# Two-layer hybrid encoder: layer 1's probabilities times values as plain fp32 products instead of three split products

## The chip, the cores and the metric

The kernel runs on one core of one Trainium2 chip. The metric is the device time of one execution in microseconds (us). A core has several engines with instruction queues of their own: TensorE (PE in the profile, its weight loads PEld), VectorE (DVE), ScalarE (ACT), GpSimd (POOL), and SyncE (SP), whose queue here issues the DMAs. Each queue is worked off in the order that was fixed when the kernel was built; an instruction that has to wait holds up what stands behind it on the same engine.

## The reference

The input x is 2048 x 1024, float32. Layer 0 is an attention layer of two mixers (a sliding window and a chunked attention with a position bias) with an input and an output projection; the change does not touch it. Layer 1 is differential attention with 8 heads, each with two queries and keys of 64 numbers and one value of 128:

```python
q1, q2, k1, k2 = ...            # projected, RMS-normed, rotated
s1, s2 = (q1 @ k1.T) / 8, (q2 @ k2.T) / 8     # chunk-causal mask: key chunk <= query chunk
a = softmax(s1) - lam * softmax(s2)
o = a @ v                        # per head: 2048 x 2048 times 2048 x 128
o = rms_norm(o, subln_g) * (1 - lambda_init)
y = (o * silu(gate)) @ w_out     # and x + y
```

The change is about `o = a @ v` and about how v is kept between the projection and that product.

## The kernel before

The work of layer 1 has two stages. The first (`_project`, lines 224 to 488) norms x, splits x and the weights into a high and a low part, and projects. The second (`_mix1`, lines 845 to 1187) does the attention, the gate projection and the output projection, woven into one another.

**Split products.** A float32 number is kept as two tiles of type fp32r: H, the rounded copy, and L, the difference to the original. A product of two such numbers is three fp32r products, HH + HL + LH, which add up in the same PSUM bank (`mm3`, lines 211 to 216, and lines 954 to 956 by hand). H is made by an ACT copy, L by a subtraction on DVE or POOL.

**Values in the projection.** The columns of v are the two groups of kind "cv" (line 291), each of 512 columns. For each of 16 blocks of 128 rows, ACT copies the PSUM bank into vH (line 483), DVE subtracts to vL (line 484), and two DMAs on SP's queue store both to HBM (lines 485 and 486): 32 of each in all. After the projection, `load_v` (lines 1026 to 1035) fetches for a head and a block of 512 keys one tile of vH and one of vL, with a DMA each, from a pool of four places for each.

**Scores.** `scores` (line 880) takes a head h and a block b of 512 queries. For each of the 4 rows of 128 queries and both softmaxes, and each chunk of up to 512 keys, PE makes a score bank with two products (lines 901 and 902; there are 4 score banks), DVE takes the row maximum (line 905), ACT the exponential into an SBUF tile (line 908). The tiles are named P0 (19 places, pool `pp`) and P1 (6 places). POOL scales both by their softmax sums and adds them (lines 924, 933, 934; every fifth time DVE does the last step, line 931). The result stays in the P0 tile and is the 128 x 512 piece of `a`; the P1 tile comes free.

**Values in the attention.** `values` (line 937) takes, for each of the (b + 1) * 4 tiles of 128 keys, the pieces of `a` of the 4 query rows, transposes them on PE (line 947) into a PSUM bank (2 banks, tag "tr"), lets ACT copy the bank to ptH (line 950) and DVE subtract to ptL (line 951), each with 3 places, and adds three products to the one output bank O (lines 954 to 956). In the block on the diagonal the later key tiles meet fewer queries, so the width falls from 512 to 384, 256 and 128. Over 8 heads and 4 blocks there are 320 key tiles, 224 of them 512 wide and 32 of each smaller width. `gate` (line 965) takes the finished bank: a copy, the norm with a sum over partitions by a plain fp32 product of the squares with a matrix of ones (line 981), and the gate.

**The order.** `pace` (line 48) runs the scores of one (head, block) ahead of the values of an earlier one by `LAG1` units (30 to 36), and lets the side work follow by a table (`STAGES1`): 256 steps of the gate projection (line 1059), then the output projection (line 1082). The order of (head, block) is: all heads with blocks 0 and 1, then all heads with block 2, then all with block 3. The last part of the output projection follows when the last head is done.

Of the kernel before, what the change touches and what calls it, by code (L numbers as in the profile page):

```python
# [10 lines left out]
F32 = mybir.dt.float32  # L11
F32R = mybir.dt.float32r
AF = mybir.ActivationFunctionType
ALU = mybir.AluOpType
# [4 lines left out]
P = 128  # L19
# [12 lines left out]
def f32(ap):  # L32
    return ap.bitcast(F32)
# [52 lines left out]
class Trunk:  # L86
# [16 lines left out]
    def scratch(self):  # L103
        dram = self.ctx.enter_context(self.tc.tile_pool(name="scr", bufs=1, space=DRAM))

        def d(name, shape):
            return dram.tile(shape, F32, tag=name, name=name)

        self.s0 = {
            "aqH": d("aqH", [4, P, S]), "aqL": d("aqL", [4, P, S]),  # L110
            "akH": d("akH", [1, P, S]), "akL": d("akL", [1, P, S]),
            "av": d("av", [S, 2 * 192]),
            "bqH": d("bqH", [4, P, S]), "bqL": d("bqL", [4, P, S]),
            "bkH": d("bkH", [4, P, S]), "bkL": d("bkL", [4, P, S]),
            "bv": d("bv", [S, 8 * 128]),
            "g": d("g0", [D, S]),
            "woH": d("wo0H", [KT, P, D]), "woL": d("wo0L", [KT, P, D]),
        }
        self.s1 = {
            "qH": d("qH", [8, P, S]), "qL": d("qL", [8, P, S]),  # L120
            "kH": d("kH", [8, P, S]), "kL": d("kL", [8, P, S]),
            "vH": d("vH", [S, D]), "vL": d("vL", [S, D]),
            "g": d("g1", [D, S]), "o": d("o1", [D, S]),
            "hH": d("hH", [KT, P, S]), "hL": d("hL", [KT, P, S]),
            "woH": d("wo1H", [KT, P, D]), "woL": d("wo1L", [KT, P, D]),
            "wgH": d("wgH", [8, P, KT, P]), "wgL": d("wgL", [8, P, KT, P]),
        }
        self.x1 = d("x1", [S, D])
# [95 lines left out]
    def _project(self, es, layer):  # L224
# [194 lines left out]
        for half in range(2):  # L419
# [13 lines left out]
            for gi, (kind, c0, width, o) in enumerate(groups):  # L433
                w = ready or weights(c0, width)
                ready = None
                if gi >= self.AHEAD:
                    next(ahead, None)
                for bi, b in enumerate(blocks):
                    if kind == "gate":
                        for c in range(4):  # L440
                            if half == 1 and gi == len(groups) - 1 and bi * 4 + c >= 8 - self.LATE:
                                self.late.append((b, c, w, h[bi], o["r0"]))
                                continue
                            ps = pmm.tile([P, 512], F32, tag="mm", name=n + "mg")
                            for k in range(KT):
                                self.mm3(
                                    ps, w[0][k][:, c * P:(c + 1) * P], w[1][k][:, c * P:(c + 1) * P],
                                    h[bi][0][:, k, :], h[bi][1][:, k, :], k == 0, k == KT - 1,
                                )
                            gt = self.yp.tile([P, 512], F32, tag="xr", name=n + "gt", bufs=2)  # L450
                            nc.scalar.activation(gt, ps, AF.Exp, scale=-1.0)
                            nc.scalar.activation(gt, gt, AF.Ln, bias=self.one)
                            nc.scalar.activation(gt, gt, AF.Exp, scale=-1.0)
                            nc.vector.tensor_tensor(gt, ps, gt, ALU.mult)
                            nc.sync.dma_start(
                                s["g"][o["r0"] + c * P:o["r0"] + (c + 1) * P, b * BLK:(b + 1) * BLK], gt
                            )
                        continue
                    xs = []
                    for j in range(NTB):  # L460
                        t = b * NTB + j
                        tok = slice(t * P, (t + 1) * P)
                        ps = project_tile(h[bi], j, w, width)
                        if kind == "qk":
                            xs.append(normed(ps, 8, o["tab"], t))
                        elif kind == "akv":
                            xs.append(normed(ps, 2, o["tab"], t))
                            vt = sb.tile([P, 2, 192], F32R, tag="sq", name=n + "vt")
                            pv = ps[:, 128:256].rearrange("p (h d) -> p h d", d=HD)
                            nc.scalar.activation(vt[:, :, 0:64], pv, AF.Copy)  # L470
                            nc.vector.tensor_tensor(vt[:, :, 64:128], pv, f32(vt[:, :, 0:64]), ALU.subtract)
                            nc.scalar.activation(vt[:, :, 128:192], pv, AF.Copy)  # L472
                            nc.sync.dma_start(s["av"][tok, :].rearrange("p (h c) -> p h c", h=2), f32(vt))
                        elif kind == "bv":
                            vt = xp.tile([P, 4, 4, HD], F32R, tag="vb", name=n + "vb", bufs=2 - layer)
                            pv = ps.rearrange("p (h e d) -> p h e d", h=4, e=2)
                            nc.scalar.activation(vt[:, :, 0::3, :], pv, AF.Copy)
                            nc.vector.tensor_tensor(vt[:, :, 1:3, :], pv, f32(vt[:, :, 0::3, :]), ALU.subtract)
                            nc.sync.dma_start(s["bv"][tok, :], f32(vt).rearrange("p a e d -> p (a e d)"))
                        else:  # L480
                            vH = gp.tile([P, 512], F32R, tag="vH", name=n + "vH")
                            vL = gp.tile([P, 512], F32R, tag="vL", name=n + "vL")
                            nc.scalar.activation(vH, ps, AF.Copy)
                            nc.vector.tensor_tensor(vL, ps, f32(vH), ALU.subtract)
                            nc.sync.dma_start(s["vH"][tok, o["c0"]:o["c0"] + 512], f32(vH))
                            nc.sync.dma_start(s["vL"][tok, o["c0"]:o["c0"] + 512], f32(vL))
                    if xs:
                        pairs_out(xs, 4 if kind == "qk" else 1, b, o)

# [355 lines left out]
    def _mix1(self, es):  # L845
# [5 lines left out]
        ld = pool("ld", 2)  # L851
        yp = pool("y", 2 * KT)
        vp = pool("v", 4)
        pp = pool("pp", 19)
        kp = pool("kp", 4)
        sb = pool("sb", 2)
        NS, NTR, NO, NM = self.BANKS1
# [22 lines left out]
        def scores(h, b, q, K, res, then):  # L880
# [4 lines left out]
            for j in range(NTB):  # L885
# [9 lines left out]
                for m in range(2):  # L895
                    chunks = []
                    for z, (c, ce) in enumerate(cuts):
# [5 lines left out]
                        if ce == nk:  # L903
                            nc.vector.memset(ps[0:HD, wd - 64:], NEG)
                        nc.vector.tensor_reduce(nm[:, m, z:z + 1], ps, AX.X, ALU.max, negate=True)  # L905
                        chunks.append((sb if m else pp).tile([P, 512], F32, tag=f"P{m}", name=n + f"P{m}", bufs=6 if m else None))
                        acc = la[:, m, z:z + 1] if nb > 1 else l[:, m:m + 1]
                        nc.scalar.activation(chunks[z][:, :wd], ps, AF.Exp, bias=nm[:, m, z:z + 1], accum_out=acc)  # L908
                        then(j, m, z)
# [27 lines left out]
        def values(h, b, res):  # L937
# [3 lines left out]
            for kt in range(nkt):  # L941
# [3 lines left out]
                kk = (kt % 4) * P  # L945
                for j in range(j0, NTB):
                    nc.tensor.transpose(tp[:, (j - j0) * P:(j - j0 + 1) * P], us[j][kt // 4][:, kk:kk + P], self.ident)  # L947
                H = sb.tile([P, 512], F32R, tag="ptH", name=n + "ptH", bufs=3)
                L = sb.tile([P, 512], F32R, tag="ptL", name=n + "ptL", bufs=3)
                nc.scalar.activation(H[:, :wd], tp[:, :wd], AF.Copy)  # L950
                nc.vector.tensor_tensor(L[:, :wd], tp[:, :wd], f32(H[:, :wd]), ALU.subtract)  # L951
                o = O[:, j0 * P:]
                vH, vL = (v[:, kk:kk + P] for v in res["v"][kt // 4])
                mm(o, vH, H[:, :wd], start=(kt == 0), stop=False, skip_group_check=True)  # L954
                mm(o, vL, H[:, :wd], start=False, stop=False, skip_group_check=True)  # L955
                mm(o, vH, L[:, :wd], start=False, stop=(kt == nkt - 1), skip_group_check=True)  # L956
                if kt == 2:
                    while normal:
                        normal.pop(0)()
# [65 lines left out]

        def load_v(h, i):
            tok = slice(i * BLK, (i + 1) * BLK)
            vs = []
            for part in ("vH", "vL"):
                v = vp.tile([P, BLK], F32R, tag=part, name=n + part)  # L1030
                nc.sync.dma_start(
                    f32(v).rearrange("p (t c) -> p t c", t=NTB), s[part][tok, h * P:(h + 1) * P].rearrange("(t p) c -> p t c", p=P)
                )
                vs.append(v)
            return vs

        room = self.last_hidden
        ended = set()
# [64 lines left out]
        def projected_last():  # L1103
# [7 lines left out]
                pairs.append((t[:, 0, :], t[:, 1, :]))  # L1111
            for i in range(4):
                pairs.append([
                    pl.tile([P, BLK], F32R, tag=tag, name=n + "w" + tag, bufs=6 if tag == "P1" else None)
                    for pl, tag in tags[1][2 * i:2 * i + 2]
                ])
            for k in range(KT):
# [110 lines left out]
```

## Time and profile before

| | before |
|---|---|
| median of 3 runs | 2894.28 us (2891.87 to 2897.59) |
| the profiled execution | 2896.36 us |
| its span, first to last instruction | 2894.3 us |
| mean granted TensorE clock over the span | 0.974 |
| PE busy in the span | 2709.4 us |
| DMA, whole kernel | 549.01 MB |
| projection of layer 1, about | 1195 to 1782 us of the span |
| attention of layer 1 with gate and output projection, about | 1782 to 2894 us |

How to read the profile: a group's line gives the source line, the engine, the operation, the tiles (output<-inputs, with a letter ahead for the stage: p1 is the projection of layer 1, c its attention), the shape and the number of instructions, then busy time and mean duration of one, then the idle time of the engine just before them and what ended most of it. So `cptL<-ctr,cptH` is line 951. A matrix product lasts longer in the record than the distance to the next one, because its way through the array overlaps with that of the next; the cost of one in a dense run is the distance between starts. A plain fp32 product is recorded as two MATMULs. In a table of windows the columns are busy time and count of each engine, the granted TensorE clock, the share of DMA time and GB/s.

### The profile page before, as it was taken

The numbers are of one execution on the slowest core, as the hardware profiler recorded it, in microseconds if no ns is written. First come the engines' busy times: TensorE is split into PE (matmuls) and PEld (weight loads), VectorE is DVE, ScalarE is ACT, GpSimd is POOL, SyncE is SP. The second block draws the span as 40 slices with busy tenths as digits, with TensorE's granted clock in tenths as the row PEclk, the third lists the DMA queues.
The fourth block names the chain that finished last, engine by engine and source line by source line (L and its number), as shares of the span: only waits on it lengthen the run. The fifth ranks groups of instructions, "written<-read, shape, count | busy, mean of one in ns | idle before, by whom it ended". The sixth has DMA issues, their size and how long they took to land. (4 is left out here: it accounts for less than half of the span.)

```text
span 2894.3 us, 45144 instructions
## 1 busy us (share of the span) xinstructions
PE 2709.4 (94%) x13704; PEld 2239.5 (77%) x13704; DVE 1970.7 (68%) x4875; ACT 1593.4 (55%) x4135; POOL 1588.1 (55%) x1740
## 2 busy tenths in 40 slices
PE   7999999999899998999999998998999999898999
PEld 5888888887788887777788887776777777676777
DVE  7752385257788875598638842578888888676772
ACT  4443543367766664343343322577776767666762
POOL 3541251334535353367645741567787878877872
PEclk9999999999999999999999999999999999899999
DMA  5673343738976765557884455978778777465553
GB/s 161 221 240 138 117 136 127 222 112 227 235 185 185 189 182 151 207 198 248 268 294 148 126 180 155 283 227 230 206 205 234 190 219 223 138 181 165 154 166 114
DMA packets 398722, 549.01 MB, mean 190 GB/s; under 512 B 46480, under 2 KB 178320, under 8 KB 398480
## 3 DMA queue, kind: packets, MB, share of 16 engines
q1 hardware_dynamic: 398480, 546.14, 63.3%
q8 instruction: 109, 1.79, 0.3%
q14 instruction: 133, 1.09, 0.1%
HBM read 380.58 MB, written 165.41 MB: 189 GB/s over the span
## 5 line engine op out<-in xcount | busy, mean ns | idle before, releaser
L908 ACT ACTIVATE cP<-cS,cnm 128x512 f32<-128x512 f32 (+3 forms) x640 | 399.3, 631 | 152.1 <-DVE cnm L905 109.0
L905 DVE TENSOR_REDUCE cnm<-cS 128x1 f32<-128x512 f32 (+3 forms) x640 | 373.8, 600 | 59.6 <-PE cS L902 54.5
L924 POOL TENSOR_SCALAR cP<-cP,crl,ce 128x512 f32<-128x512 f32 (+3 forms) x288 | 213.8, 755 | 207.3 <-DVE crl L919 73.4
L214 PE MATMUL p1mm<-p1wH,p1hH 128*128 128x512 f32 x768 | 302.8, 396 | 0.7 <-ACT p1wH L308 0.7
L215 PE MATMUL p1mm<-p1wL,p1hH 128*128 128x512 f32 x768 | 302.9, 395 | 0.4 <-POOL p1wL L310 0.4
L216 PE MATMUL p1mm<-p1wH,p1hL 128*128 128x512 f32 x768 | 303.1, 395 | 0.0
L901 PE MATMUL cS<-ck,cqd 128*128 128x512 f32 (+3 forms) x640 | 264.4, 416 | 40.2 <-ACT cP L908 28.1
L310 POOL TENSOR_TENSOR p0wL<-p0ws,p0wH 128x512 fp32r<-128x512 f32 (+1 forms) x124 | 148.7, 1229 | 269.0 <-ACT p0wH L308 266.7
L934 POOL TENSOR_TENSOR cP<-cP,cP 128x512 f32<-128x512 f32 (+3 forms) x256 | 286.6, 1141 | 1.2
L214 PE MATMUL p0mm<-p0wH,p0hH 128*128 128x512 f32 (+1 forms) x640 | 239.6, 376 | 4.7 <-ACT p0vt L472 4.0
L310 POOL TENSOR_TENSOR p1wL<-p1ws,p1wH 128x512 fp32r<-128x512 f32 x128 | 167.5, 1328 | 138.6 <-ACT p1wH L308 97.6
L902 PE MATMUL cS<-ck,cql 128*128 128x512 f32 (+3 forms) x640 | 236.3, 373 | 5.3 <-DMA cql<-qL 5.3
L216 PE MATMUL p0mm<-p0wH,p0hL 128*128 128x512 f32 (+1 forms) x640 | 239.2, 374 | 1.9 <-DVE p0hL L336 1.9
L215 PE MATMUL p0mm<-p0wL,p0hH 128*128 128x512 f32 (+1 forms) x640 | 239.8, 375 | 0.0
L951 DVE TENSOR_TENSOR cptL<-ctr,cptH 128x512 fp32r<-128x512 f32 (+1 forms) x320 | 190.8, 599 | 53.4 <-ACT cptH L950 52.7
L950 ACT ACTIVATE cptH<-ctr 128x512 fp32r<-128x512 f32 (+1 forms) x320 | 170.3, 538 | 80.2 <-PE ctr L947 78.9
L901 PEld LDWEIGHTS cS<-ck,cqd 128*128 128x128 f32 x640 | 123.1, 193 | 79.0 <-ACT cP L908 53.6
L947 PE MATMUL ctr<-ident,cP 128*128 128x128 f32 x1088 | 177.9, 278 | 6.4 <-POOL cP L934 3.9
L933 POOL TENSOR_SCALAR cP<-cP,crl,ce 128x512 f32<-128x512 f32 (+3 forms) x230 | 177.4, 781 | 5.1 <-DVE crl L920 5.1
L215 PEld LDWEIGHTS p1mm<-p1wL,p1hH 128*128 128x128 f32 x768 | 145.3, 189 | 29.8 <-POOL p1wL L310 0.8
L214 PEld LDWEIGHTS p1mm<-p1wH,p1hH 128*128 128x128 f32 x768 | 145.4, 189 | 29.6 <-ACT p1wH L308 1.0
L216 PEld LDWEIGHTS p1mm<-p1wH,p1hL 128*128 128x128 f32 x768 | 145.3, 189 | 29.2 <-issue 0.2
(311 smaller groups left out, 7744.7 us busy)
## 6 DMA issues: line engine op xcount, KB each, us to landing
p1ws<-in_od_w_in_dram SPq DMA_DIRECT2D x56, 512.0 KB, 4.9
p0ws<-in_ev_w_in_dram SPq DMA_DIRECT2D x48, 512.0 KB, 4.5
ck<-kH SPq DMA_DIRECT2D x144, 128.0 KB, 4.1
ck<-kL SPq DMA_DIRECT2D x144, 128.0 KB, 4.2
cvH<-vH SPq DMA_DIRECT2D x72, 256.0 KB, 4.6
cvL<-vL SPq DMA_DIRECT2D x72, 256.0 KB, 4.4
cqd<-qH SPq DMA_DIRECT2D x128, 128.0 KB, 4.6
cql<-qL SPq DMA_DIRECT2D x128, 128.0 KB, 4.7
```

The source lines that it names most:

```text
L214: mm(ps, aH, bH, start=first, stop=False)
L215: mm(ps, aH, bL, start=False, stop=False)
L216: mm(ps, aL, bH, start=False, stop=last)
L310: low.tensor_tensor(l[:, :width], ws[:, k, :width], f32(h[:, :width]), ALU.subtract)
L901: mm(ps, qd[:, m, js], kt[:, :wd], start=True, stop=False)
L902: self.anchor = mm(ps, ql[:, m, js], kt[:, :wd], start=False, stop=True).ins
L905: nc.vector.tensor_reduce(nm[:, m, z:z + 1], ps, AX.X, ALU.max, negate=True)
L908: nc.scalar.activation(chunks[z][:, :wd], ps, AF.Exp, bias=nm[:, m, z:z + 1], accum_out=acc)
L924: nc.gpsimd.tensor_scalar(p1, p1, rl[:, 0:1], e1, ALU.mult, ALU.mult)
L934: nc.gpsimd.tensor_tensor(p1, p1, p2, ALU.add)
L947: nc.tensor.transpose(tp[:, (j - j0) * P:(j - j0 + 1) * P], us[j][kt // 4][:, kk:kk + P], self.ident)
L951: nc.vector.tensor_tensor(L[:, :wd], tp[:, :wd], f32(H[:, :wd]), ALU.subtract)
```

## The change

Values are stored and loaded once, as float32. The transposed probabilities are copied once, as float32, and not split: for two of three key tiles by ACT and for every third by DVE. One plain fp32 product takes the place of the three fp32r products. The copy has 6 places where ptH and ptL had 3 each. The P0 tiles get 20 places instead of 19, the P1 tiles 8 instead of 6; the value tiles have 4 places where vH and vL had 4 each.

```diff
-            "vH": d("vH", [S, D]), "vL": d("vL", [S, D]),
+            "v": d("v", [S, D]),
...
-                            vH = gp.tile([P, 512], F32R, tag="vH", name=n + "vH")
-                            vL = gp.tile([P, 512], F32R, tag="vL", name=n + "vL")
-                            nc.scalar.activation(vH, ps, AF.Copy)
-                            nc.vector.tensor_tensor(vL, ps, f32(vH), ALU.subtract)
-                            nc.sync.dma_start(s["vH"][tok, o["c0"]:o["c0"] + 512], f32(vH))
-                            nc.sync.dma_start(s["vL"][tok, o["c0"]:o["c0"] + 512], f32(vL))
+                            vt = gp.tile([P, 512], F32, tag="v", name=n + "v", bufs=3)
+                            nc.scalar.activation(vt, ps, AF.Copy)
+                            nc.sync.dma_start(s["v"][tok, o["c0"]:o["c0"] + 512], vt)
...
-        pp = pool("pp", 19)
+        pp = pool("pp", 20)
...
-                        chunks.append((sb if m else pp).tile([P, 512], F32, tag=f"P{m}", name=n + f"P{m}", bufs=6 if m else None))
+                        chunks.append((sb if m else pp).tile([P, 512], F32, tag=f"P{m}", name=n + f"P{m}", bufs=8 if m else None))
...
-                H = sb.tile([P, 512], F32R, tag="ptH", name=n + "ptH", bufs=3)
-                L = sb.tile([P, 512], F32R, tag="ptL", name=n + "ptL", bufs=3)
-                nc.scalar.activation(H[:, :wd], tp[:, :wd], AF.Copy)
-                nc.vector.tensor_tensor(L[:, :wd], tp[:, :wd], f32(H[:, :wd]), ALU.subtract)
-                o = O[:, j0 * P:]
-                vH, vL = (v[:, kk:kk + P] for v in res["v"][kt // 4])
-                mm(o, vH, H[:, :wd], start=(kt == 0), stop=False, skip_group_check=True)
-                mm(o, vL, H[:, :wd], start=False, stop=False, skip_group_check=True)
-                mm(o, vH, L[:, :wd], start=False, stop=(kt == nkt - 1), skip_group_check=True)
+                T = sb.tile([P, 512], F32, tag="pt", name=n + "pt", bufs=6)
+                if kt % 3:
+                    nc.scalar.activation(T[:, :wd], tp[:, :wd], AF.Copy)
+                else:
+                    nc.vector.tensor_copy(T[:, :wd], tp[:, :wd])
+                v = res["v"][kt // 4][:, kk:kk + P]
+                mm(O[:, j0 * P:], v, T[:, :wd], start=(kt == 0), stop=(kt == nkt - 1), skip_group_check=True)
...
-            vs = []
-            for part in ("vH", "vL"):
-                v = vp.tile([P, BLK], F32R, tag=part, name=n + part)
-                nc.sync.dma_start(
-                    f32(v).rearrange("p (t c) -> p t c", t=NTB), s[part][tok, h * P:(h + 1) * P].rearrange("(t p) c -> p t c", p=P)
-                )
-                vs.append(v)
-            return vs
+            v = vp.tile([P, BLK], F32, tag="v", name=n + "v")
+            nc.sync.dma_start(
+                v.rearrange("p (t c) -> p t c", t=NTB), s["v"][tok, h * P:(h + 1) * P].rearrange("(t p) c -> p t c", p=P)
+            )
+            return v
...
-                    pl.tile([P, BLK], F32R, tag=tag, name=n + "w" + tag, bufs=6 if tag == "P1" else None)
+                    pl.tile([P, BLK], F32R, tag=tag, name=n + "w" + tag, bufs=8 if tag == "P1" else None)
```

## The prediction

> **What bounds the kernel now.** The page comes first: PE is busy 94% of the span. The table of windows comes next, since that share is a mean over stages.
>
> ```profile
> PE 2709.4 (94%) x13704; PEld 2239.5 (77%) x13704; DVE 1970.7 (68%) x4875; ACT 1593.4 (55%) x4135; POOL 1588.1 (55%) x1740
> ```
>
> ```profile
> 1195.00:1782.00 587.00, 572.14 (x2664) 470.88 (x2664) 402.90 (x701) 219.33 (x495) 332.97 (x256) 0.99 0.63 206
> 1782.00:2182.00 400.00, 359.44 (x1737) 288.31 (x1738) 298.54 (x832) 277.69 (x800) 276.07 (x335) 0.94 0.80 232
> 2182.00:2482.00 300.00, 285.40 (x1426) 229.63 (x1424) 252.00 (x564) 215.59 (x602) 228.96 (x259) 0.99 0.73 205
> 2482.00:2682.00 200.00, 171.74 (x793) 134.06 (x793) 133.52 (x309) 128.97 (x352) 156.72 (x168) 0.90 0.59 168
> 2820.00:2894.00 74.00, 68.89 (x326) 54.25 (x324) 22.14 (x36) 17.70 (x32) 19.29 (x18) 1.00 0.37 119
> ...
> 1782.00:2894.00 1112.00, 1016.91 (x4928) 812.06 (x4928) 813.10 (x1978) 737.35 (x2048) 787.78 (x896) 0.96 0.68 197
> ```
>
> The projection of layer 1 (first row) is PE's: 572 of 587 us. The attention stage (last row) is where the change acts. There PE is still the busiest engine, 1017 of 1112 us, but VectorE, GpSimd and ScalarE are at 73, 71 and 66%, and the granted clock falls to 0.94 and 0.90 in two of its parts. Recorded busy time overstates PE, as a product's record reaches into the next. The timeline has the real distances.
>
> ```profile
> 2008.55 0.40 PE L955 MATMUL cO<-cptH,cvL 128*128 128x512 f32 x1
> 2008.79 0.39 PE L956 MATMUL cO<-cptL,cvH 128*128 128x512 f32 x1
> 2009.02 0.39 PE L214 MATMUL cG<-p1hH,cwH 128*128 128x512 f32 x1
> 2009.25 0.39 PE L215 MATMUL cG<-p1hL,cwH 128*128 128x512 f32 x1
> ```
>
> ```profile
> 2012.02 1.02 PE L981 MATMUL cms<-csq,ones 128*128 128x512 f32 x2
> 2012.88 0.60 PE L947 MATMUL ctr<-ident,cP 128*128 128x128 f32 x4
> ```
>
> An fp32r product 512 wide takes 0.23 us from start to start (2008.79, 2009.02, 2009.25), though its record lasts 0.39. The only plain fp32 product of the kernel, the sum of squares, takes 2012.88 - 2012.02 = 0.86 us for its two MATMULs. Four transposes of 128 columns last 0.60 us with 0.278 each (row L947 below), so they follow each other by (0.60 - 0.278)/3 = 0.11 us: per column the same as one of those two MATMULs, 0.43/4.
>
> ```profile
> L902 PE MATMUL cS<-ck,cql 128*128 128x512 f32 x448 | 179.5, 401 | 0.0
> L947 PE MATMUL ctr<-ident,cP 128*128 128x128 f32 x1088 | 177.9, 278 | 6.4 <-POOL cP L934 3.9 <-DVE cptL L951 1.5 <-DVE cP L931 0.8
> L954 PE MATMUL cO<-cptH,cvH 128*128 128x512 f32 x224 | 97.9, 437 | 3.3 <-ACT cot L971 2.6 <-ACT cptH L950 0.4
> L981 PE MATMUL cms<-csq,ones 128*128 128x512 f32 x64 | 32.8, 594 | 1.3 <-ACT csq L973 1.3
> L214 PE MATMUL cG<-p1hH,cwH 128*128 128x512 f32 x256 | 106.1, 415 | 3.5 <-DMA cwH<-wgH 3.1 <-ACT cgt L1068 0.3
> ```
>
> With widths 384, 256 and 128 counted by their share of 512 (64 of each in the scores, 32 in the values), PE's real work in the stage is: scores 2 x (448 + 96) x 0.23 = 250, transposes 1088 x 0.11 = 120, values 3 x (224 + 48) x 0.23 = 188, gate projection 3 x 256 x 0.23 = 177, output projection the same 177 (32 tiles of 24 products), sums of squares 64 x 0.43 = 28. That is 940 of 1112 us. A clock of 0.96 loses at most 44 us, and 37 if it is lost evenly over work and idle time (times 940/1112). So some 135 us are real idle time of PE, and the question is how much of it the change gives back. The waits name the larger part:
>
> ```profile
> PE cS L901 <- ACT cP L908: 28.1, 38, 3.7
> PE cO L956 <- DVE cptL L951: 15.3, 11, 4.3
> PE ctr L947 <- DVE cptL L951: 1.5, 3, 0.9
> PE cO L954 <- ACT cptH L950: 0.4, 2, 0.2
> ```
>
> ```profile
> DVE cptL L951 <- ACT cptH L950: 52.7, 42, 9.2
> ACT cP L908 <- DVE cnm L905: 109.0, 103, 4.8
> ACT cptH L950 <- PE ctr L947: 78.9, 66, 6.8
> ACT cP L908 <- POOL cP L934: 7.5, 10, 2.7
> SPq L1031 <- PE cO L955: 93.3, 19, 14.1
> ```
>
> Two things stop PE: a score bank that the exponential has not yet freed, and the low part of the probabilities. Behind the first stands a loop: the exponential waits for the row maximum, the maximum stands in VectorE's queue behind a subtraction, that waits for ScalarE's copy, and the copy for PE's transposes. To each of PE's waits comes the end of the product ahead of it, recorded 0.39 - 0.23 = 0.16 us longer than it holds PE.
>
> **The products.** One plain product costs 0.86 us, the three that it replaces 3 x 0.23 = 0.69. Over 224 + 48 = 272 full widths that is 272 x 0.17 = **+46 us** of PE work, with nothing to hide it while PE is the bound; in idle time that ends at a fixed moment it would be absorbed. The weight loads fall from 960 to 640 and lie under products, as they do now.
>
> On this the Trainium skill, FP8 and Floating Point Precision, TensorE Precision Notes, says that true FP32 takes 4 passes through the array, while reduced FP32 is cut to what the array takes natively. By that rule a product would cost 4 x 0.23 = 0.92 us, the term would be 272 x 0.23 = 63 us, and the rule speaks against the change; the trace agrees in kind, with 0.86 / 0.23 = 3.7 passes.
>
> **The copies.** The subtractions go. The prices of full widths and the totals:
>
> ```profile
> L951 DVE TENSOR_TENSOR cptL<-ctr,cptH 128x512 fp32r<-128x512 f32 (+1 forms) x320 | 190.8, 599 | 53.4 <-ACT cptH L950 52.7
> L950 ACT ACTIVATE cptH<-ctr 128x512 fp32r<-128x512 f32 (+1 forms) x320 | 170.3, 538 | 80.2 <-PE ctr L947 78.9
> L905 DVE TENSOR_REDUCE cnm<-cS 128x1 f32<-128x512 f32 x448 | 300.8, 680 | 57.4 <-PE cS L902 54.5
> L484 DVE TENSOR_TENSOR p1vL<-p1mm,p1vH x32: 682/692/693, 1416.2 to 1779.8; 128x512 fp32r<-128x512 f32 x32
> ```
>
> Key tiles 0, 3, 6 and so on go to VectorE: 2, 3, 4 and 6 of the four blocks, 15 of 40 per head, 120 of 320. A VectorE copy out of PSUM is not in the trace. Two operations that read a PSUM bank of 512 have 680 and 692 ns, so I take the 599 ns mean of the subtraction: 120 x 0.60 = 72 us; it could be half that, and hardly more. VectorE loses 190.8 - 72 = 119 us of 813 (to 62% of the stage), ScalarE 120 x 0.54 = 65 of 737 (to 60%). None of this is on PE's path by itself. It counts through the waits.
>
> The low part's wait goes: 15.3 + 11 x 0.16 + 1.5 + 3 x 0.16 = 19 us. Late next is the copy itself; its wait today is 0.4 us, but only because the later wait covers it, so I give back 3 (bounds 0 and 19): **-16**.
>
> The wait for score banks is 28.1 + 38 x 0.16 = 34 us. The subtraction no longer stands ahead of the maximum; a VectorE copy does in its place for one key tile in three, and it waits for the transposes directly. 8 places for P1 and 20 for P0 also take the exponential out of POOL's shadow (7.5 us). Bounds 0 and -34; VectorE and ScalarE lose 15% and 9% of their work and one hop of the loop, which is more than a trimming, so nearer the far end: **-20**.
>
> Of the 135 us, the two waits above explain 53. Some 80 are stalls hidden in the overlap of records, DMA waits and hand-overs at O. Bounds 0 and -40 (half of them); a seventh: **-12**. The clock's 37 us go with the stalls, as the parts with the lower clock are those with the lower PE share. The three returns so far are 48 of the 135 us of pauses, about a third; a third of 37 is 13, and since not every pause lowers the clock I take **-10** (0 to -25).
>
> **Values in HBM.** In the projection VectorE loses 32 x 0.69 = 22 us and SP 32 stores. PE is at 97% there and waits for none of these, so 0; if PE's cover went, it would be at most the 22. In the attention 72 loads fall away:
>
> ```profile
> cvL<-vL SPq DMA_DIRECT2D x72, 256.0 KB, 4.4
> ```
>
> SP's queue stands 93 us at value loads that wait for a free place, with the q, k and gate loads behind them. A place still comes free with the last product that reads it, so that stays. Fewer issues and 18.9 MB less can only help; 0, within the remainder above.
>
> **The sum:** 46 - 16 - 20 - 12 - 10 = -12 us. The profiled execution took 2896.4 us for a span of 2894.3, 2.1 above the median, less than the three runs' spread; I make no difference between them: 2896 - 12 = **2884 us**.
>
> **Rivals.** *PE becomes the plain bound (slower).* Place: the in-order PE queue of the stage, above all in 2182 to 2482 and after 2820, where PE is 95 and 93% busy already. If the score bank is late because of the order of the queues and not of VectorE's load, only the low part's wait returns: 46 - 16 = +30, 2926 us. It decides from where less than 46 us of the 172 of idle and lost clock come back. For it: to end at 2884, PE must do 940 + 46 us of work in 1100, 90%, against 85% now. Against it: VectorE, the stage's second engine, is at 84% (252 of 300) in that dense part and is the one relieved. Chance 0.33, and with a part of the returns it reaches down to 2901.
>
> *Gain and price cancel (no change).* Returns of 40 to 52 us. It has a chance of 0.20, with a price of four full passes in it (0.04): 2884 + 17 = 2901 at the edge of it. That the product is not what it says, and is built of cheap passes, would take the 46 away; the row of line 981 speaks against it, under 0.02, within the gains.
>
> *The loop was the bound.* All of the score wait goes, two thirds of the clock's loss and half of the 40: 46 - 16 - 34 - 25 - 20 = -49, 2847 us. For it: 109 us in which the exponential waited for the maximum. Against it: GpSimd, not relieved, is at 78% (157 of 200) in 2482 to 2682. Chance 0.12.
>
> **How the numbers follow.** The forecast has 0.35, with its own range of 2866 to 2888. A measurement tells 0.2%, some 6 us, from no change. Faster is 0.35 + 0.12 = 0.47, same 0.20, slower 0.33. For 8 in 10 the range goes from 2852, short of the loop's full gain, to 2918, short of the bound's full price.
>
> **What would show it.** Right: 640 MATMULs in the product's line in place of 960, with 0.86 us per pair; VectorE near 694 and ScalarE near 672 us busy in the stage; no wait for a low part; the score-bank wait below 15 us; a clock of 0.97 or more. Wrong: a score-bank wait that stays near 28 us with VectorE idle, a product far from 0.86 us, or new waits of PE on the copies above 10 us.

## The result, and the profile after

| | before | after |
|---|---|---|
| median | 2894.74 us (11 runs, 2889.87 to 2899.74) | 2868.88 us (11 runs, 2859.53 to 2886.69) |
| ratio to before | | 0.9909, 95% interval 0.9889 to 0.9929 |
| span of the profiled execution | 2894.3 us | 2867.1 us |
| mean granted TensorE clock | 0.974 | 0.982 |
| DMA, whole kernel | 549.01 MB | 521.68 MB |

The kernel became faster by 26 us (0.9%; by the interval 21 to 32 us). The forecast was 12 us less.

In the kernel after, the score products stand in lines 898 and 899, the row maximum in 902, the exponential in 905, the transposes in 944, the two copies in 947 (ACT) and 949 (DVE), and the product in 951. These are stretches of the table of windows (columns as before: busy time and count of PE, PEld, DVE, ACT and POOL, then clock, DMA share, GB/s):

```profile
1195.00:1782.00 587.00, 569.22 (x2665) 468.23 (x2663) 377.58 (x668) 218.54 (x494) 334.67 (x256) 1.00 0.59 193
1782.00:2182.00 400.00, 375.84 (x1702) 281.67 (x1703) 279.31 (x797) 272.95 (x791) 289.87 (x348) 0.96 0.78 227
...
2482.00:2682.00 200.00, 185.09 (x795) 130.68 (x796) 139.07 (x282) 124.57 (x340) 161.13 (x175) 0.95 0.46 138
...
1782.00:2900.00 1118.00, 1028.93 (x4608) 754.73 (x4608) 724.59 (x1778) 688.82 (x1928) 791.18 (x896) 0.97 0.61 178
```

In the projection the change moved next to nothing: by 1782 us TensorE had done 2665 products, against 2664 before, though VectorE lost 25 us there. In the attention TensorE has more work than before and is nevertheless done sooner: its share of 1782 to 2182 rose from 359 to 376 of 400 us, of 2482 to 2682 from 172 to 185 of 200, and the granted clock there from 0.94 and 0.90 to 0.96 and 0.95. VectorE's busy time in the stage fell from 813 to 725 us, ScalarE's from 737 to 689; GpSimd kept its 790. The groups and the timeline show the new operations.

```profile
L951 PE MATMUL cO<-cpt,cv 128*128 128x512 f32 (+3 forms) x640 | 288.6, 539 | 12.3 <-DVE cpt L949 9.6 <-ACT cpt L947 2.3 <-DVE ctop L911 0.2
L947 ACT ACTIVATE cpt<-ctr 128x512 f32<-128x512 f32 (+3 forms) x200 | 106.7, 535 | 60.4 <-PE ctr L944 59.9
L949 DVE COPY cpt<-ctr 128x512 f32<-128x512 f32 (+2 forms) x120 | 72.5, 604 | 37.3 <-PE ctr L944 36.8
```

```profile
2602.47 1.02 PE L951 MATMUL cO<-cpt,cv 128*128 128x512 f32 x2
2603.33 0.60 PE L944 MATMUL ctr<-ident,cP 128*128 128x128 f32 x4
```

The product takes 2603.33 - 2602.47 = 0.86 us, as the sum of squares did in the kernel before. The waits of the stage:

```profile
PE cS L898 <- ACT cP L905: 12.0, 10, 3.4
PE cO L951 <- DVE cpt L949: 9.6, 4, 7.2
PE cO L951 <- ACT cpt L947: 2.3, 1, 2.3
```

```profile
ACT cP L905 <- DVE cnm L902: 170.8, 169, 8.8
```

The score-bank wait of TensorE fell from 28.1 us in 38 waits to 12.0 in 10, and the wait for the low part, 15.3 us, gave place to 11.9 us of waits for the copies. The exponential's own wait for the row maximum grew, from 109.0 to 170.8 us, while the kernel became faster: ScalarE has less to do and stands idle more often. The idle time of an engine that is not the bottleneck is no loss.

### The profile page after: what moved, and what is told of

It is laid out like the page before. It is cut to its first block, busy times and chain, and to the rows that moved or that the text cites. A ratio compares the mean times of both kernels' runs of the same rounds, so it can differ in the third digit from the quotient of the medians.

```text
span 2867.1 us, 43943 instructions
## 1 busy us (share of the span) xinstructions
PE 2717.2 (95%) x13384; PEld 2177.3 (76%) x13384; DVE 1856.3 (65%) x4643; ACT 1544.8 (54%) x4015; POOL 1595.3 (56%) x1740
## 2 busy tenths in 40 slices
DMA packets 356092, 521.68 MB, mean 182 GB/s; under 512 B 44816, under 2 KB 139792, under 8 KB 355856
## 4 chain that ended last, share of the span: by engine, by line
PE 71%; DVE 8%; DMA 7%; ACT 4%; issue 2%; POOL 2%; SPq 1%; DVEq 0%; ACTq 0%; POOLq 0%
PE cO L951 7%; PE p1mm L216 5%; PE p1mm L215 5%; PE p1mm L214 5%; PE cS L898 4%; PE cS L899 4%; PE ctr L944 3%; PE p0mm L214 2%; PE p0mm L216 2%; PE p0mm L215 2%; PE com L214 2%; PE com L215 2%; PE com L216 2%; PE mom L214 2%; PE mom L215 2%
## 5 line engine op out<-in xcount | busy, mean ns | idle before, releaser
L905 ACT ACTIVATE cP<-cS,cnm 128x512 f32<-128x512 f32 (+3 forms) x640 | 397.6, 628 | 191.5 <-DVE cnm L902 170.8
L921 POOL TENSOR_SCALAR cP<-cP,crl,ce 128x512 f32<-128x512 f32 (+3 forms) x288 | 215.8, 762 | 186.9 <-DVE crl L916 99.4
L951 PE MATMUL cO<-cpt,cv 128*128 128x512 f32 (+3 forms) x640 | 288.6, 539 | 12.3 <-DVE cpt L949 9.6
L944 PEld LDWEIGHTS ctr<-ident,cP 128*128 128x128 f32 x1088 | 137.6, 142 | 115.0 <-issue 60.9
L930 POOL TENSOR_SCALAR cP<-cP,crl,ce 128x512 f32<-128x512 f32 (+3 forms) x230 | 181.4, 800 | 0.7 <-DVE crl L917 0.7
```

Of the source, the lines that this page charges most:

```text
L921: nc.gpsimd.tensor_scalar(p1, p1, rl[:, 0:1], e1, ALU.mult, ALU.mult)
L951: mm(O[:, j0 * P:], v, T[:, :wd], start=(kt == 0), stop=(kt == nkt - 1), skip_group_check=True)
```

## The experiments

Every kernel is given as its ratio to the kernel before on the same chip; 0.1% is 2.9 us. Differences of two such ratios carry some 0.2 to 0.3%.

**1. The subtraction left out, in the kernel before.**

```diff
-                L = sb.tile([P, 512], F32R, tag="ptL", name=n + "ptL", bufs=3)
...
-                nc.vector.tensor_tensor(L[:, :wd], tp[:, :wd], f32(H[:, :wd]), ALU.subtract)
...
-                mm(o, vH, L[:, :wd], start=False, stop=(kt == nkt - 1), skip_group_check=True)
+                mm(o, vH, H[:, :wd], start=False, stop=(kt == nkt - 1), skip_group_check=True)
```

> The kernel before, with the subtraction on VectorE left out and the third product made with H again (the low part of the probabilities is left out of the result). TensorE keeps its three cheap products. Theory (the subtraction costs through the waits, about 60 to 75 us of TensorE idle time and lost clock): 2820 to 2835 us. Rival 1 (the new places for P0 and P1 make the gain, which this kernel does not have): 2880 us or more. Rival 2 (the halved value traffic makes the gain): 2880 us or more as well.

Measured: 0.9858 (0.9835 to 0.9881), 41 us less. TensorE does the same work as before in this run, so the 41 us are idle time and clock that it got back; they are less than expected, and the far end of the score-bank and clock terms was not reached. Both rivals are refuted as the sole cause.

**2. Three cheap products in place of the plain one, in the kernel after.**

```diff
-                T = sb.tile([P, 512], F32, tag="pt", name=n + "pt", bufs=6)
+                T = sb.tile([P, 512], F32R, tag="pt", name=n + "pt", bufs=6)
...
-                mm(O[:, j0 * P:], v, T[:, :wd], start=(kt == 0), stop=(kt == nkt - 1), skip_group_check=True)
+                for i in range(3):
+                    mm(O[:, j0 * P:], v, T[:, :wd], start=(kt == 0 and i == 0), stop=(kt == nkt - 1 and i == 2), skip_group_check=True)
```

The value tile is of type fp32r too.

> The kernel after, with its one copy and its places, but three fp32r products of the same two tiles in place of the plain fp32 product (the low parts are left out of the result). Only TensorE's work differs from the kernel after, by about 48 us less. Theory (TensorE is the bound after the change, so the price of the plain product is paid nearly in full): 2820 to 2832 us. Rival (the price is absorbed in waits that end at moments not set by TensorE): 2855 to 2869 us.

Measured: 0.9830 (0.9813 to 0.9848), against 0.9909 for the kernel after: 0.79%, 23 us with some 8 either way. Neither theory holds: of the 46 us of added TensorE work about half lengthens the kernel, and the other half must fall into time in which TensorE stood idle.

**3. The places put back, in the kernel after.**

```diff
-        pp = pool("pp", 20)
+        pp = pool("pp", 19)
...
-                        chunks.append((sb if m else pp).tile([P, 512], F32, tag=f"P{m}", name=n + f"P{m}", bufs=8 if m else None))
+                        chunks.append((sb if m else pp).tile([P, 512], F32, tag=f"P{m}", name=n + f"P{m}", bufs=6 if m else None))
```

> The kernel after with the places of before: 19 for P0 and 6 for P1. Theory (the places are a side matter): 2869 to 2876 us. Rival 1 (the places make the gain): 2888 to 2900 us.

Measured: 0.9900 (0.9882 to 0.9918), the same as the kernel after. The places did nothing that can be measured.

**4. VectorE's load kept, with the places put back.**

```diff
-                if kt % 3:
-                    nc.scalar.activation(T[:, :wd], tp[:, :wd], AF.Copy)
-                else:
-                    nc.vector.tensor_copy(T[:, :wd], tp[:, :wd])
+                nc.scalar.activation(T[:, :wd], tp[:, :wd], AF.Copy)
+                L = sb.tile([P, 512], F32, tag="ptL", name=n + "ptL", bufs=2)
+                nc.vector.tensor_tensor(L[:, :wd], tp[:, :wd], T[:, :wd], ALU.subtract)
```

> The kernel after with places 19 and 6, every copy on ScalarE as before, and VectorE subtracting as before into a tile that nobody reads, so that its load and the hop from ScalarE to VectorE are there again and only the wait of TensorE for the low part is not. It stands against the run with the places put back. Theory (VectorE's load and the hop make the waits for score banks): 15 to 35 us above that run, 2888 to 2910 us. Rival (only TensorE's own wait for the low part counted): within 8 us of that run.

Measured: 0.9947 (0.9928 to 0.9966), 0.47% or 14 us above the run with the places put back, with some 8 either way: just under the theory's span, and not clear of the rival's. Nor is all of it VectorE's load, since ScalarE got VectorE's 120 copies as well. Run 7 has them there without the subtraction and is at 0.9934; against it the subtraction adds 0.13%, 4 us, which is not clear of noise. And with that load and the dearer product the kernel is still 15 us faster than before. Something else had to pay; runs 5, 6, 9 and 10 are about that.

**5. The low part made but not read, in the kernel before.**

```diff
-                mm(o, vH, L[:, :wd], start=False, stop=(kt == nkt - 1), skip_group_check=True)
+                mm(o, vH, H[:, :wd], start=False, stop=(kt == nkt - 1), skip_group_check=True)
```

> The kernel before, with the subtraction on VectorE kept, but the third product made with H, so that nobody reads the low part (which is left out of the result). VectorE's and ScalarE's load and order stay; only TensorE's wait for the low part goes. Theory as predicted (that wait itself is the smaller part, VectorE's load the larger): 16 to 22 us below before, a ratio of 0.992 to 0.994. Rival (the wait is nearly all of it): 33 to 41 us below, a ratio of 0.986 to 0.989, within 0.3% of the run without the subtraction.

Measured: 0.9972 (0.9957 to 0.9987), 8 us, less than the theory gave the wait. But the run does not take all of TensorE's waiting for the subtraction away. The subtraction still reads the transposes' bank, and the transposes' wait for it grew from 1.5 us to 9.8:

```profile
PE ctr L947 <- DVE cptL L951: 9.8, 4, 4.0
```

So the other 33 of the 41 us that the subtraction costs in run 1 are VectorE's load together with its hold on that bank.

**6. The values loaded a second time, with the places put back.**

```diff
+            v2 = vp.tile([P, BLK], F32, tag="v2", name=n + "v2")
+            nc.sync.dma_start(
+                v2.rearrange("p (t c) -> p t c", t=NTB), s["v"][tok, h * P:(h + 1) * P].rearrange("(t p) c -> p t c", p=P)
+            )
             return v
```

> The kernel after with the old places, and with a second load of every value tile into a tile that nobody reads, so that the 72 DMAs and 18.9 MB that the change took away are there again. It stands against the run with the places put back, whose ratio was 0.990. Theory (the value traffic is a side matter): 0 to 6 us more, 0.990 to 0.992. Rival (SyncE's queue and the DMA engines held TensorE up through the values): 10 to 15 us more, 0.9935 to 0.995.

Measured: 1.0019 (1.0003 to 1.0036), 1.2% or 34 us more than without the second load, beyond both expectations. The rows: the first part of the stage, a wait of SyncE's queue, and TensorE's new waits.

```profile
1782.00:2182.00 400.00, 359.52 (x1564) 266.19 (x1564) 252.72 (x739) 254.42 (x726) 263.41 (x320) 0.93 0.90 251
```

```profile
SPq L1028 <- DMA cv<-v: 22.2, 27, 3.7
```

```profile
PE cS L898 <- DMA cqd<-qH: 7.2, 3, 4.2
PE cS L899 <- DMA cql<-qL: 7.2, 7, 2.5
```

The loss lies in 1782 to 2182: DMA share 0.90, TensorE back at 360 of 400 us, as in the kernel before. But the second tiles have no reader, and SyncE's queue stood 22 us until an earlier load into the same place had landed; in the kernel before its waits of this kind come to under 3 us. So the run is not a clean measure of the traffic; runs 9 and 10 are.

**7. All copies on ScalarE, in the kernel after.**

```diff
-                if kt % 3:
+                if True:
```

> The kernel after with all 320 copies on ScalarE: VectorE loses 120 copies of 0.69 us at full width, ScalarE gets 120 of 0.60. Theory (VectorE's queue ahead of the row maximum is what still holds the score banks): 5 to 10 us faster than the kernel after, a ratio of 0.987 to 0.989. Rival (the two engines' loads count alike, and ScalarE frees the score banks): 0 to 10 us slower, 0.991 to 0.9945.

Measured: 0.9934 (0.9916 to 0.9952), 7 us above the kernel after, with intervals that overlap. The theory of a faster kernel falls. That the two engines' loads count alike fits, but the 7 us are not clear of no change.

**8. Every third last step on VectorE, in the kernel after.**

```diff
-    COMB = 5
+    COMB = 3
```

> The kernel after with every third instead of every fifth last step of the probabilities on VectorE (107 of 320 instead of 64): GpSimd, busy 791 us in the stage, loses about 90 us, VectorE, 725 us, gets about 45. Theory (TensorE is the bound, with short waits on all others): within 6 us of the kernel after, 0.989 to 0.993. Rival (GpSimd, the one engine that the change did not relieve, is the second bound): 8 to 20 us faster, 0.984 to 0.988.

Measured: 0.9848 (0.9826 to 0.9869), 0.61% or 18 us faster than the kernel after, and 44 us faster than before. The rival holds: GpSimd, the engine that the change did not relieve, was worth relieving. (The trace counts 106 such steps on VectorE.)

```profile
1782.00:2900.00 1118.00, 1022.24 (x4598) 750.25 (x4597) 737.05 (x1854) 686.07 (x1924) 734.86 (x812) 0.98 0.60 177
```

VectorE and GpSimd are level at 737 and 735 us, and the clock in the stage is 0.98. GpSimd lost 56 us of busy time and VectorE got 12, both less than expected.

**9 and 10. One value load in place of two, in the kernels of runs 5 and 1.** The second value load is left out in the attention; the store stays.

```diff
-                vH, vL = (v[:, kk:kk + P] for v in res["v"][kt // 4])
+                vH = vL = res["v"][kt // 4][0][:, kk:kk + P]
...
-            for part in ("vH", "vL"):
+            for part in ("vH",):
```

> The kernel before with the subtraction kept but unread, as in the run of that kind (ratio 0.9972), and in the attention only the high part of the values loaded, all three products made with it (both low parts are left out of the result). Against that run only 72 DMAs of 256 KB are gone. Theory A (the halved value loads are worth some 30 us, as the doubled loads suggested): a ratio of 0.985 to 0.989. Theory B (the doubled loads were slow because SyncE's queue stood at the unread tiles' places; the traffic itself is a side matter): 0.993 to 0.998.

> The kernel before without the subtraction, as in the run of that kind (ratio 0.9858), and in the attention only the high part of the values loaded (both low parts are left out of the result). Theory A (value loads are worth some 30 us on their own): 0.974 to 0.978. Theory B (a side matter, and with VectorE relieved even less): 0.981 to 0.986. If the loads help much with VectorE loaded and little with it relieved, the two gains overlap.

Measured: 0.9868 (0.9849 to 0.9888) and 0.9835 (0.9817 to 0.9853). With VectorE loaded, the 72 loads are worth 0.9972 - 0.9868 = 1.04%, 30 us: theory A. With VectorE relieved they are worth 0.9858 - 0.9835 = 0.23%, 7 us, which is not clear of the intervals: theory B. The two gains overlap. Together they give 0.9972 - 0.9835 = 1.37%, 40 us, where the sum of each alone would be 33 + 30 = 63. The rows of run 5, two loads, and then of run 9, one load:

```profile
1782.00:2182.00 400.00, 366.62 (x1787) 296.27 (x1787) 304.93 (x854) 285.06 (x825) 280.94 (x338) 0.95 0.82 236
...
2482.00:2682.00 200.00, 177.20 (x833) 138.96 (x834) 140.83 (x314) 130.70 (x355) 160.39 (x176) 0.92 0.53 155
```

```profile
SPq L1031 <- PE cO L956: 105.7, 32, 11.9
```

```profile
1782.00:2182.00 400.00, 372.80 (x1849) 300.23 (x1850) 311.50 (x872) 292.85 (x847) 295.33 (x353) 0.98 0.79 230
...
2482.00:2682.00 200.00, 186.37 (x907) 148.16 (x906) 151.54 (x344) 140.36 (x383) 163.11 (x179) 0.95 0.48 147
```

```profile
SPq L1031 <- PE cO L956: 107.3, 24, 15.1
```

SyncE's queue stands as long for free value places in both (105.7 and 107.3 us), so that standing is not what the loads cost. TensorE's share rises in both stretches and the clock with it, from 0.95 and 0.92 to 0.98 and 0.95. Which of the rest it is, the time to issue 72 DMAs or their share of the DMA engines, no run told apart. It also stays open why run 6, with VectorE relieved, lost 34 us where runs 1 and 10 differ by 7: its queue's waits and the plain product both differ.

**11. Every second last step on VectorE, in the kernel after.** The edit is that of run 8 with a 2.

> The kernel after with every second last step of the probabilities on VectorE (160 of 320): GpSimd some 110 us less than with every third, VectorE some 55 more. Theory (with every third the two are level at 735 to 737 us, so VectorE now becomes the later one): 3 to 15 us slower than with every third, 0.986 to 0.990. Rival (GpSimd is still the second bound): 0.980 to 0.983.

Measured: 0.9863 (0.9845 to 0.9880). Not clear of run 8, and no further gain: the step stops paying where the two engines are level.

**12. Every third last step on VectorE, in the kernel before.** The edit is that of run 8.

> The kernel before with every third last step of the probabilities on VectorE. Theory (the room on VectorE that the change made is what this step uses; before, VectorE is at 813 us and GpSimd at 788): no gain or a loss, 0.999 to 1.008. Rival (GpSimd's relief pays by itself): 0.992 to 0.996, as with the kernel after.

Measured: 0.9889 (0.9870 to 0.9909). The theory falls plainly: this one number gives the kernel before as much as the whole change did, although VectorE was its second busiest engine. The room on VectorE was not needed. On the kernel after the same number gives 0.6% rather than 1.1%: these gains overlap, too. Seen the other way, on a kernel that has this number already the change adds 0.41%, 12 us (run 8 against run 12).

## Why the prediction was right, and where it was not

**The direction and the range were right**, and so was the picture of the stage: TensorE takes on work, the others lose some, and the idle time that comes back outweighs the price. The forecast of 2884 was 15 us too high. Its price of 46 us was 23, while its returns of 58 us were nearer: runs 10 and 2, which do not pay the price, gain 48 and 49. That the returns come so near is partly luck, as the loads, which the sum put at 0, are among them.

**The products: the price right, its cover not.** The 0.86 us were exact. That nothing would hide them was not: 46 us of work cost 23 (run 2). Two other pairs of kernels that differ mainly in the product give 23 (runs 9 and 4) and 29 us (runs 10 and 7). The prediction had said that in idle time they would be absorbed, and then counted them in full. The rule of four passes in the Trainium skill (FP8 and Floating Point Precision, TensorE Precision Notes) has its measure here: 0.86 us is 3.7 times an fp32r product's 0.23.

**The low part's wait, -16: probably too large.** Run 5 gives 8, with the transposes still waiting. The prediction gave back 3 us for the copies' own wait, and the profile shows 11.9: "late next" was larger than it was sized. New waits on the copies above 10 us were named as a sign of being wrong, and this sign came. It decides little: in run 3, which is as fast, they are 5.7 us.

**The score banks, the hidden stalls and the clock, -20, -12 and -10: the relief is shown, its path is not.** What VectorE's load is worth, with its hold on the transposes' bank, is 33 us with two value loads (runs 1 and 5), and with one 10 (runs 9 and 10, 0.33%) or 4 (runs 4 and 7), against 42 in the three terms. VectorE's copies cost the 604 ns that were taken. The score-bank wait fell to 12.0 us, below the 15 that was named as the mark. But this row does not carry the gain. Here it is in runs 1, 3 and 10, in this order:

```profile
PE cS L901 <- ACT cP L908: 24.0, 26, 3.3
PE cS L898 <- ACT cP L905: 20.2, 20, 4.6
PE cS L901 <- ACT cP L908: 27.6, 27, 5.4
```

Run 3 is as fast as the kernel after. Runs 1 and 10 are faster, with no subtraction left on VectorE, and the wait stands nearly where it stood before, at 28.1. So the mark was met, but each row is one execution, and through which of TensorE's pauses VectorE's relief pays stays open. Whether the higher clock (0.974 to 0.982 over the span) is a cause or follows from fewer pauses was not told apart either. VectorE was to be near 694 us busy in the stage and is at 725; by the sums of the groups it lost what was reckoned, 190.8 - 72.5 = 118 us, but busy time counts overlapping records once.

**The values in HBM, 0: right for the projection, wrong for the attention.** It was argued from SyncE's standing at full places. Run 9 gives 30 us for the 72 loads while VectorE is loaded, and runs 1 and 10 give 7 when it is not. The change takes away both, so its 40 us cannot be split between them. No row of TensorE's waits in the profile before carries the loads' 30 us. It may be that a late load moves scores, maxima and exponentials, and that TensorE's wait is then put down to whatever came last; that is argued and not shown.

**The sum again, by runs:** the wait 8, VectorE's relief and the loads together 40 (runs 5 and 10), the price 23 the other way: 25 us, against the 26 measured. The places add nothing (run 3). From the other end it closes as well: run 10, the kernel before without the subtraction and with one load, is at 0.9835, and run 2, the kernel after without the price, at 0.9830.

**The rivals.** TensorE as the plain bound is refuted, as half of its added work was covered. That the loop was the bound is refuted as well: its 49 us are what is left after the price of 46, so it has returns of 95 us in it, and runs 1 and 10, which do not pay the price, gave 41 and 48. GpSimd, which the prediction named only as a reason against that gain, was worth relieving in both kernels (runs 8 and 12).

## What to carry to other kernels

Here TensorE was busy nine tenths of the stage, and three engines and the DMA stood at two thirds to three quarters; relieving VectorE, the DMA queue or GpSimd each paid, and the gains overlapped. In such a stage, measure them in pairs before adding them up. A resource whose waits are short in the table of waits is not free, a row of waits can shrink without the time following it, and added work on the busiest engine is not paid in full while it has idle gaps. Before a costly change, try the number that shifts work between the other engines: here one digit on the old kernel was worth as much, and with the change it makes the best version, 0.9848.

## What the runs showed of the hardware that was not expected

Taking 72 loads of 256 KB out of a stage at 68% DMA share gave 30 us with VectorE loaded and 7, not clear of noise, with it relieved. A load into a tile that nobody reads still held SyncE's queue, 22 us in 27 waits, until an earlier load into the same place had landed.
